# The response matrices on SyncE's queue, and the first MLP's last two down chunks as one seven-product pair

## The chip, the cores and the metric

The kernel runs on one core of one Trainium2 chip. The metric is the device time of one execution in microseconds, lower being better. Before the change three runs gave 2769.85, 2770.20 and 2771.99 us, a median of 2770.2 us.

Five engines work side by side, each in the order of its own instructions: TensorE (PE in the profile, with its weight loads as PEld), VectorE (DVE), ScalarE (ACT), GpSimd (POOL) and SyncE (SP). Transfers between main memory and the on-chip buffer are issued by an engine, here by SyncE or GpSimd, and carried out by 16 DMA engines that all queues share.

## The reference, cut to what matters

Two decoder layers on 256 tokens of width 2048, all in float32. Each layer is `x + mixer(norm(x))`, then `x + memory_attention(norm(x), norm(mem))`, then `x + mlp(norm(x))`; a final norm follows. Two places matter here: the MLP of layer 0 and the mixer of layer 1 right behind it.

```python
def squared_relu_mlp(h, w_up, w_down):          # 2048 -> 8192 -> 2048
    return jnp.square(jax.nn.relu(h @ w_up)) @ w_down

def s5_glu(h, w_in, ...):                       # mixer of layer 1
    u = (h @ w_in).reshape(bsz, seq, 128, 16)   # 128 groups of 16 channels
    ...                                         # 64 complex states a group
    states = lax.associative_scan(combine, (a, bu), axis=0)
    y = jnp.einsum('gcp,sbgp->bsgc', cmat, states).real + d_skip * u
    y = gelu(y)
    val, gate = jnp.split(y @ w_out + b_out, 2, axis=-1)
    return val * sigmoid(gate)
```

## The kernel before

**Products.** Every float32 weight tile of 512 KB (two k tiles of 128 rows by 512 columns, `KB = 2`, `NB = 512`) is loaded by SyncE into a buffer `wraw` (`wload`, L117; four buffers, and a fifth one in the first MLP), cut by ScalarE into a high part `whi` (L103) and by VectorE into a low part `wlo` (L104; three buffers each), and then used by TensorE in 12 matmuls: two k tiles, two token halves, three partial products (high by high, low by high, high by low). `tick` (L83) runs after each such tile. Work that is to be emitted some tiles later is handed to `at(delay, fn)` (L78), which counts in ticks.

**The order on the engines** isn't the order of the source: a scheduler places the instructions by priority, which is the order of emission unless `later` or `high_priority` changes it. `issue_after(self.fed)` keeps a SyncE transfer behind the last weight load that was emitted.

**The first MLP** (`mlp`, L678, layer 0). The 8192 hidden features come in four blocks. For each block the up product makes four chunks of 512 features (`gemm_feat`, L163, squared ReLU at L697), and the down product adds four chunks `n` of 512 output columns onto `x`. In layer 0 each down chunk is `gemm_hid` (L901): 8 weight tiles, 96 matmuls, then two `gather` calls (L720) that add the two token halves to `x`. In the last block, `nxt.start()` (L718) makes the buffer of the next norm, and `nxt.chunk(x, n)` (L744) squares, turns and scales chunk `n` of `x` one tick after it is complete. So the next mixer finds `hT`, its transposed and split input.

**Seven products instead of eight.** The second MLP and the attention's output product already do two chunks at once in `gemm_seven` (L784): of 16 k tiles, four are taken as a 2 by 2 block product with seven instead of eight half-tile products. Before them VectorE forms differences of raw weight tiles (`run`), and sums of activations (`token_sums`, L748: four sums, then the split). Each product has 6 matmuls. Partial results are copied out by `keep` and added by `gather`. The pair holds two accumulators from its start.

**Activation buffers.** `self.act` has two buffers of 32 KB a partition, for whatever is tagged `act`. During the first MLP one holds its input `hT`, and the other `room`, the workspace of the state-space preparation (`ssm_prep`, L1004), which runs beside the MLP and ends with the writes of `Kd` (L1226).

**The state-space mixer** (`s5`, L1259). The input product takes 32 weight tiles (`b_w_in`), four chunks `n` of 8 tiles each, then the output product takes 64 (`b_w_out`). Beside it, per chunk `n`, run small products with matrices that the preparation wrote to main memory: `pq` (4 transfers of 512 KB), `qq` (4 of 512 KB) and the response matrices `dq`. A response matrix is a tile of 128 partitions with a triangle in it, so it is fetched (L1293) as four transfers of 32, 64, 96 and 128 KB, each into 32 partitions:

```python
load(bass.AP(tensor=kd.tensor, offset=kd.offset + 6 * P,
             ap=[[P, 2], [(2 * T - 1) * P, 16], [1, 2 * (h + 1) * P]]),
     t[32 * h:32 * h + 32, 2 * (3 - h) * P:])
```

There are four such matrices a chunk, 16 transfers, 1.25 MB, and 64 transfers in all. They have one set of four tiles (`resp`, L1276), so those of chunk `n` can come only when the products of chunk `n - 1` have read theirs. `load` issues on GpSimd unless `stream` is true, and for `dq` it never is: `pq` and `dq` are GpSimd's, `qq` and the weights SyncE's. `follow(n)` (L1412) hands the work of chunk `n` to `at`; it is called at tick 8(n + 1) of the mixer. The products with `dq` (L1384) and `qq` (L1392) are in `outputs(n, half)`, 14 and 16 ticks later.

Of the kernel before, what the change touches and what calls it, by code (L numbers as in the profile page):

```python
# [9 lines left out]
F32 = mybir.dt.float32  # L10
F32R = mybir.dt.float32r
# [5 lines left out]
P = 128  # L17
# [21 lines left out]
class Trunk:  # L39
# [638 lines left out]
    def mlp(self, x, layer, cur, nxt):  # L678
        nc, a, tc = self.nc, self.a, self.tc
        wu, wd = a["f_w_up"][layer], a["f_w_down"][layer]  # L680
        hT = cur.act
        with tc.tile_pool(name="ml", bufs=4, reuse_waits="tile") as mp:
            r2 = mp.tile([P, 32 if layer else 24], F32, name="r2", bufs=1)[:, 0:2]
            ws = lambda: mp.tile([P, KB * NB], F32, name="ws", bufs=4)
            run = lambda: mp.tile([P, KB * NB], F32, name="run", bufs=1)
            kept = lambda i: more[:, 6 + i // 2, i % 2 * NB:i % 2 * NB + NB]
            self.fifth = None if nxt.closing else mp
            for b in range(DFF // D):
                hid = []
                for n in range(NCH):  # L690
                    h = mp.tile([P, 4, S], F32R, name="hh")
                    l = mp.tile([P, 4, S], F32R, name="hl")
                    rs = []
                    for i in range(2):
                        r = mp.tile([P, 2, S], F32, name="r", bufs=2)
                        self.gemm_feat(hT, wu, 2 * (NCH * b + n) + i, r)
                        nc.vector.scalar_tensor_tensor(out=r, in0=r, scalar=0.0, in1=r, op0=ALU.max, op1=ALU.mult)  # L697
                        self.split(h[:, 2 * i:2 * i + 2], l[:, 2 * i:2 * i + 2], r)
                        rs.append(r)
                    hid.append((h, l))  # L700
                    if nxt.closing and n == 0:
                        sums = []
                    if nxt.closing and n < 2:
                        sums.append(self.token_sums(ws(), lambda: mp.tile([P, 4, 2, P], F32R, name="sums", bufs=4), *rs))
                    if nxt.closing and n == NCH - 2:
                        more = self.act.tile([P, 8, KB * NB], F32, name="more", tag="act")
                        ahead = [self.block_ahead(more, wd, 2 * j, b * KT, j) for j in range(1 if b == DFF // D - 1 else 2)]
                        ahead[0][-2]()
                if nxt.closing:
                    ahead[0][-1](0, 1, 2)  # L710
                if nxt.closing:
                    own = lambda: mp.tile([P, KB * NB], F32R, name="own", bufs=2)
                    nxt.room = lambda: mp.tile([P, 2, NB], F32, name="g", tag="ws", bufs=4)
                if b == 0:
                    rstd = cur.rstd()
                    nc.vector.tensor_tensor(out=r2, in0=rstd, in1=rstd, op=ALU.mult)
                if b == DFF // D - 1 and not nxt.closing:
                    nxt.start()  # L718

                def gather(t, n, part, cs=None):  # L720
                    xc = x[:, t, cs or slice(n * NB, (n + 1) * NB)]
                    nc.vector.scalar_tensor_tensor(out=xc, in0=part, scalar=r2[:, t:t + 1], in1=xc,
                                                   op0=ALU.mult, op1=ALU.add)

                for n in range(NCH):
                    end = b == DFF // D - 1
                    if nxt.closing and not (end and n >= NCH - 2):
                        if n % 2 == 0:
                            self.gemm_seven((ws, run, kept), lambda kt, t: [f[:, kt % 4, t * P:(t + 1) * P]
                                                                            for f in hid[kt // 4]],  # L730
                                            sums, wd, n, b * KT, gather, own=own, ahead=ahead[n // 2],
                                            then=ahead[1] if n == 0 and len(ahead) > 1 else None)
                            if end:
                                nxt.start()
                    elif nxt.closing and end and n == NCH - 1:
                        self.gemm_last(hid, wd, n, b * KT, lambda t, acc: nxt.finish(x, t, lambda cs: gather(
                            t, n, acc[:, cs.start - n * NB:cs.stop - n * NB], cs)))
                        break
                    else:
                        acc = self.gemm_hid(hid, wd, n, b * KT)  # L740
                        for t in range(2):
                            gather(t, n, acc[:, t, :])
                    if end:
                        self.at(4 + n if nxt.closing and n < 2 else 1, lambda n=n: nxt.chunk(x, n))  # L744

            self.fifth = None

# [256 lines left out]
    def ssm_prep(self, pool):  # L1004
# [32 lines left out]
        bbs = [home(4 * 2 * 16).rearrange("p (g k c) -> p g k c", g=4, k=2) for _ in range(4)]  # L1037
        qts = [home((T + 1) * 4 * 16).rearrange("p (w g c) -> p w g c", g=4, c=16) for _ in range(4)]
        pos = [home(4 * 2 * 64).rearrange("p (t r s) -> p t r s", t=4, r=2) for _ in range(4)]
        kds = [home(NL * 2 * 16).rearrange("p (w i c) -> p w i c", i=2, c=16) for _ in range(2)]  # L1040

        def cmul(orr, oi, ar, ai, br, bi):
# [49 lines left out]
        def zoh():  # L1092
            lr, li = e["lr"], e["li"]
            pr, pi = e["pw"][1]
            fr, fi = pool.tile(W, F32, name="fr", tag="w2"), pool.tile(W, F32, name="fi", tag="w3")
            nr, den = pool.tile(W, F32, name="nr", tag="w7"), pool.tile(W, F32, name="den", tag="w9")
            v.tensor_tensor(out=den, in0=lr, in1=lr, op=ALU.mult)
            v.tensor_tensor(out=nr, in0=li, in1=li, op=ALU.mult)
            v.tensor_tensor(out=den, in0=den, in1=nr, op=ALU.add)
            v.reciprocal(out=den, in_=den)  # L1100
            v.tensor_scalar(out=nr, in0=pr, scalar1=-1.0, scalar2=None, op0=ALU.add)
            v.tensor_scalar(out=li, in0=li, scalar1=-1.0, scalar2=None, op0=ALU.mult)
            cmul(fr, fi, nr, pi, lr, li)
            v.tensor_tensor(out=fr, in0=fr, in1=den, op=ALU.mult)
            v.tensor_tensor(out=fi, in0=fi, in1=den, op=ALU.mult)
            pt = self.ps([P, 4, P])
            for k, t in enumerate((fr, fi)):
                nc.tensor.transpose(pt[:, k, :], t, self.ident)
            nc.scalar.copy(out=F, in_=pt[:, 0:2, :])
            e["f"] = fr[:, 0:64], fi[:, 0:64]  # L1110
            lk = pool.tile([P, 2, 64], F32, name="lk")
            for k in range(2):
                nc.scalar.copy(out=lk[:, k], in_=e["f"][k])
            nc.gpsimd.dma_start(out=Ld[0], in_=lk)
            row(1)

        def row(k):
            lk = pool.tile([P, 2, 64], F32, name="lk")
            cmul(lk[:, 0], lk[:, 1], *(f[:, 0:64] for f in e["pw"][k]), *e["f"])
            nc.gpsimd.dma_start(out=Ld[k], in_=lk)  # L1120

# [137 lines left out]
    def s5(self, x, cur, nxt):  # L1259
# [3 lines left out]
        with tc.tile_pool(name="s5", bufs=2, reuse_waits="tile") as sp:  # L1263
# [17 lines left out]
            def fetch(nm, n, i, stream=False):  # L1281
# [5 lines left out]
                elif nm == "qq":  # L1287
                    t = sp.tile([P, 2, 4 * P], F32, name=nm, bufs=4)
                    load(self.Qd[4 * n + i].rearrange("l p r n -> (l p) r n"), t, stream)
                else:  # L1290
                    t, kd = resp[i], self.Kd[4 * n + i]
                    for h in range(4):
                        load(bass.AP(tensor=kd.tensor, offset=kd.offset + 6 * P,  # L1293
                                     ap=[[P, 2], [(2 * T - 1) * P, 16], [1, 2 * (h + 1) * P]]),
                             t[32 * h:32 * h + 32, 2 * (3 - h) * P:])
                ahead[nm, n, i] = t

            def chunks(n, acc):
# [113 lines left out]
            def follow(n):  # L1412
# [3 lines left out]
                for i in range(4):  # L1416
                    if n + 1 < NCH:
                        self.at(5, lambda i=i: fetch("pq", n + 1, i))
                    if n:
                        self.at(7 + late + i // 2 * 2, lambda i=i: fetch("dq", n, i))  # L1420
                        self.at(10 + late + i // 2 * 2, lambda i=i: fetch("qq", n, i, True))
                self.at(4 + late, lambda: inputs(n))
                self.at(6 + late, lambda: states(n))
                self.at(7 + late, lambda: [carry(n, 2, 15), carry(n, 4, 7, 2)])
# [8 lines left out]

            for i in range(4):
                fetch("pq", 0, i)
            for i in range(4):
                fetch("dq", 0, i)
                self.at(2 * i + 2, lambda i=i: fetch("qq", 0, i, True))
            for n in range(NCH):
                acc = self.gemm_tok(hT, a["b_w_in"], n)  # L1440
                if n == 0:
# [227 lines left out]
```

## Time and profile before

| | us |
|---|---|
| median of three runs | 2770.2 |
| the profiled execution | 2772.35 |
| its span, from the first to the last instruction | 2770.2 |
| TensorE busy | 2748.3 |
| VectorE busy | 2066.9 |
| ScalarE busy | 1426.7 |
| GpSimd busy | 184.9 |

The profile covers one execution; its span lacks 2.15 us at the two ends. "Busy" is the time in which an engine had an instruction at work. In the views of the trace, a row of the timeline has the start, the length and the number of like instructions in a row, and in square brackets the idle time before them with what ended it. A row of the windows has the busy time of each engine with the number of its instructions, the granted share of TensorE's clock, the mean busy share of the 16 DMA engines, and the rate.

### The profile page before, as it was taken

The page shows a single profiled execution, that of the slowest core. Times are in us where ns is not written, and L with a number is a line of the kernel's source. Part 1 is how long each engine was busy: PE and PEld are TensorE (multiplying, and loading weights), DVE is VectorE, ACT ScalarE, POOL GpSimd, SP SyncE. Part 2 cuts the span into 40 slices and gives each one's busy share as a digit, 9 for nine tenths or more (in the row PEclk, how much of TensorE's full clock was granted, in tenths as well). Part 3 has the DMA queues.
Part 4 walks back from the last instruction along what each step waited for, and adds up shares of the span by engine and source line. Part 5 has one row for each costly group of instructions (what it writes and reads, how often), then busy time and mean ns, then how long its engine had stood idle before and what let it go on. Part 6 is the DMA issues. An engine that isn't in the chain of part 4 may idle for free. (4 is left out here: it accounts for less than half of the span.)

```text
span 2770.2 us, 39500 instructions
## 1 busy us (share of the span) xinstructions
PE 2748.3 (99%) x14966; PEld 2325.4 (84%) x14966; DVE 2066.9 (75%) x2835; ACT 1426.7 (51%) x1822; POOL 184.9 (7%) x331
## 2 busy tenths in 40 slices
PE   9999999999999999999999999999999999999998
PEld 7888888888888888888888788888888888888887
DVE  6865757878888878787577657568767978879685
ACT  5545545655544434444566445446555655546454
POOL 0100000001011111111203100000000000000000
PEclk9999999999999999999999999999999999999999
DMA  8766566457688887886879766564556557575565
GB/s 293 231 199 214 189 193 217 152 160 238 211 281 259 262 258 257 265 259 219 235 239 284 207 203 206 188 213 156 181 165 231 180 171 241 158 246 166 176 212 160
DMA packets 194175, 593.75 MB, mean 214 GB/s; under 512 B 44096, under 2 KB 45168, under 8 KB 193472
## 3 DMA queue, kind: packets, MB, share of 16 engines
q1 hardware_dynamic: 153456, 537.46, 61.1%
q0 software_dynamic: 40000, 52.71, 6.6%
q8 instruction: 117, 1.92, 0.3%
q10 hardware_dynamic: 528, 1.06, 0.1%
q14 instruction: 74, 0.61, 0.1%
HBM read 567.51 MB, written 23.46 MB: 213 GB/s over the span
## 5 line engine op out<-in xcount | busy, mean ns | idle before, releaser
L104 DVE TENSOR_TENSOR wlo<-wraw,whi 128x1024 fp32r<-128x1024 f32 (+1 forms) x857 | 1041.0, 1220 | 434.8 <-ACT whi L103 429.0
L103 ACT CAST whi<-wraw 128x1024 fp32r<-128x1024 f32 (+1 forms) x857 | 899.4, 1051 | 800.2 <-PE acc L910 172.1
L174 PE MATMUL acc<-act,whi 128*128 128x512 f32 x3072 | 740.9, 391 | 0.6 <-DVE act L246 0.6
L174 PEld LDWEIGHTS acc<-act,whi 128*128 128x128 f32 x3072 | 563.1, 188 | 110.6 <-issue 1.4
L179 PEld LDWEIGHTS acc<-act,wlo 128*128 128x128 f32 x3072 | 395.0, 191 | 17.4 <-DVE wlo L104 1.8
L179 PE MATMUL acc<-act,wlo 128*128 128x256 f32 x3072 | 403.3, 283 | 1.3 <-DVE wlo L104 1.0
L159 PE MATMUL acc<-whi,act 128*128 128x512 f32 x1472 | 370.4, 393 | 5.6 <-ACT whi L103 5.5
L159 PEld LDWEIGHTS acc<-whi,act 128*128 128x128 f32 x1472 | 275.2, 189 | 63.6 <-ACT whi L103 6.3
L810 PE MATMUL acc<-whi,act 128*128 128x512 f32 x824 | 222.7, 392 | 0.0
L910 PE MATMUL acc<-whi,hl 128*128 128x512 f32 x544 | 212.7, 391 | 0.0
L909 PE MATMUL acc<-whi,hh 128*128 128x512 f32 x544 | 212.6, 391 | 0.0
L159 PE MATMUL acc<-wlo,act 128*128 128x512 f32 x736 | 197.9, 391 | 0.0
L810 PEld LDWEIGHTS acc<-whi,act 128*128 128x128 f32 x824 | 152.9, 188 | 35.9 <-ACT ends L846 2.2
L159 PEld LDWEIGHTS acc<-wlo,act 128*128 128x128 f32 x736 | 138.6, 188 | 28.9
L912 PE MATMUL acc<-wlo,hh 128*128 128x512 f32 x544 | 145.8, 389 | 0.0
L810 PE MATMUL acc<-wlo,act 128*128 128x512 f32 x412 | 127.2, 391 | 0.2
L190 ACT COPY r<-acc 128x512 f32<-128x512 f32 x64 | 37.6, 587 | 161.9 <-PE acc L174 161.9
L910 PEld LDWEIGHTS acc<-whi,hl 128*128 128x128 f32 x544 | 102.1, 188 | 22.2 <-issue 1.0
L810 PE MATMUL acc<-whi,hh 128*128 128x512 f32 x308 | 120.5, 391 | 0.0
L909 PEld LDWEIGHTS acc<-whi,hh 128*128 128x128 f32 x544 | 102.1, 188 | 21.4 <-issue 0.2
L912 PEld LDWEIGHTS acc<-wlo,hh 128*128 128x128 f32 x544 | 102.0, 188 | 21.4 <-issue 0.2
L810 PE MATMUL acc<-whi,hl 128*128 128x512 f32 x308 | 119.9, 389 | 0.0
(387 smaller groups left out, 2951.3 us busy)
## 6 DMA issues: line engine op xcount, KB each, us to landing
wraw<-in_f_w_up SPq DMA_DIRECT2D x256, 512.0 KB, 4.5
wraw<-in_f_w_down SPq DMA_DIRECT2D x200, 512.0 KB, 5.6
wraw<-in_x_w_q SPq DMA_DIRECT2D x64, 512.0 KB, 3.7
wraw<-in_x_w_k SPq DMA_DIRECT2D x64, 512.0 KB, 4.5
wraw<-in_b_w_out SPq DMA_DIRECT2D x64, 512.0 KB, 4.5
wraw<-in_a_w_in SPq DMA_DIRECT2D x63, 512.0 KB, 4.7
wraw<-in_x_w_o SPq DMA_DIRECT2D x48, 512.0 KB, 4.3
wraw<-in_x_w_v SPq DMA_DIRECT2D x40, 512.0 KB, 3.9
```

Source lines behind the costliest of these rows:

```text
L103: self.nc.scalar.copy(out=hi, in_=src)
L104: return self.nc.vector.tensor_tensor(out=lo, in0=src, in1=hi.bitcast(F32), op=ALU.subtract).ins
L159: nc.tensor.matmul(out[t], a[:, kt, sl], b[:, kk, :], start=st and a is ah, stop=en)
L174: nc.tensor.matmul(acc[:, f, :], hi[:, kk, sl], both[:, kt].rearrange("p a s -> p (a s)"), start=first and kk == 0, stop=last and kk == FK ...
L179: nc.tensor.matmul(acc[:, f, 0:S], lo[:, kk, sl], ah[:, kt, :], start=False, stop=last and kk == FK - 1, skip_group_check=True)
L190: nc.scalar.copy(out=dst, in_=acc[:, :, S:])
L810: mm = lambda s, m, e: nc.tensor.matmul(out, s, m, start=key not in begun, stop=e, skip_group_check=True)
L909: nc.tensor.matmul(acc[:, t, :], ah, hi[:, kk, :], start=kt == 0, stop=False)
L910: nc.tensor.matmul(acc[:, t, :], al, hi[:, kk, :], start=False, stop=False)
L912: nc.tensor.matmul(acc[:, t, :], hid[kt // 4][0][:, kt % 4, sl], lo[:, kk, :], start=False, stop=kt == KT - 1)
```

## The change

Three things are done. In the last block of the first MLP, the down chunks 2 and 3 go through `gemm_seven` as one pair; its four raw tiles are loaded into a new `act` tile `more` when chunk 1 begins, the sums of activations are formed after the block's first up chunk with `self.spare` (a stretch of `room`) as workspace, and the norm's chunk 3 is handed on with a delay of 2 ticks. In the mixer, the `dq` transfers go to SyncE's queue, and `dq` and `qq` get new ticks: for chunk 0, 6, 8, 14, 16 and three ticks after each; for the others 12 and 14, and one tick after each. Two small preparation tiles share a buffer (`w9`).

```diff
@@ mlp @@
-            ws = lambda: mp.tile([P, KB * NB], F32, name="ws", bufs=4)
-            run = lambda: mp.tile([P, KB * NB], F32, name="run", bufs=1)
+            if nxt.closing:
+                ws = lambda: mp.tile([P, KB * NB], F32, name="ws", bufs=4)
+                run = lambda: mp.tile([P, KB * NB], F32, name="run", bufs=1)
+            else:
+                ws, run = None, lambda: more[:, 4]
...
-                    if nxt.closing and n == 0:
+                    if n == 0:
                         sums = []
-                    if nxt.closing and n < 2:
-                        sums.append(self.token_sums(ws(), lambda: mp.tile([P, 4, 2, P], F32R, name="sums", bufs=4), *rs))
+                    if nxt.closing and n < 2 or not nxt.closing and n == 0 and b == DFF // D - 1:
+                        sums.append(self.token_sums(ws() if nxt.closing else self.spare, lambda: mp.tile([P, 4, 2, P], F32R, name="sums", bufs=4 if nxt.closing else 2),
+                                                    *rs))
...
                 if b == DFF // D - 1 and not nxt.closing:
+                    more = self.act.tile([P, 8, KB * NB], F32, name="more", tag="act")
+                    early = {}
                     nxt.start()
...
+                    elif end and n >= NCH - 2 and not nxt.closing:
+                        if n % 2 == 0:
+                            self.gemm_seven((ws, run, kept), lambda kt, t: [f[:, kt % 4, t * P:(t + 1) * P]
+                                                                            for f in hid[kt // 4]],
+                                            sums, wd, n, b * KT, gather, raw=early)
                     else:
+                        if end and n == 1:
+                            for i, j in ((0, 0), (0, 1), (1, 0), (1, 1)):
+                                t = early[i, j] = more[:, 2 * i + j]
+                                with tc.issue_after(self.fed):
+                                    nc.sync.dma_start(out=t.rearrange("p (k c) -> p k c", k=KB),
+                                                      in_=wd[2 + j, b * KT // KB + i])
                         acc = self.gemm_hid(hid, wd, n, b * KT)
...
-                        self.at(4 + n if nxt.closing and n < 2 else 1, lambda n=n: nxt.chunk(x, n))
+                        self.at(4 + n if nxt.closing and n < 2 else 1 if n < 3 else 2, lambda n=n: nxt.chunk(x, n))
@@ ssm_prep @@
+        self.spare = home(KB * NB)
...
-            lk = pool.tile([P, 2, 64], F32, name="lk")
+            lk = pool.tile([P, 2, 64], F32, name="lk", tag="w9")
@@ s5 @@
-                        load(bass.AP(tensor=kd.tensor, offset=kd.offset + 6 * P,
+                        load(stream=stream, src=bass.AP(tensor=kd.tensor, offset=kd.offset + 6 * P,
                                      ap=[[P, 2], [(2 * T - 1) * P, 16], [1, 2 * (h + 1) * P]]),
-                             t[32 * h:32 * h + 32, 2 * (3 - h) * P:])
+                             out=t[32 * h:32 * h + 32, 2 * (3 - h) * P:])
...
-                    if n:
-                        self.at(7 + late + i // 2 * 2, lambda i=i: fetch("dq", n, i))
-                        self.at(10 + late + i // 2 * 2, lambda i=i: fetch("qq", n, i, True))
+                for k, nm in enumerate(("dq", "qq")) if n else ():
+                    for i in range(4):
+                        self.at(12 + i // 2 * 2 + k, lambda nm=nm, i=i: fetch(nm, n, i, True))
...
-            for i in range(4):
-                fetch("dq", 0, i)
-                self.at(2 * i + 2, lambda i=i: fetch("qq", 0, i, True))
+            for k, nm in enumerate(("dq", "qq")):
+                for i in range(4):
+                    self.at((6, 8, 14, 16)[i] + 3 * k, lambda nm=nm, i=i: fetch(nm, 0, i, True))
```

More of the change, by code (lines that the diff above doesn't have):

```diff
@@ L1117, in row @@
         def row(k):
-            lk = pool.tile([P, 2, 64], F32, name="lk")
+            lk = pool.tile([P, 2, 64], F32, name="lk", tag="w9")
             cmul(lk[:, 0], lk[:, 1], *(f[:, 0:64] for f in e["pw"][k]), *e["f"])
```

## The prediction

> **What bounds the kernel now.** First the page's head and busy times, then who waited for whom on TensorE.
>
> ```profile
> span 2770.2 us, 39500 instructions
> PE 2748.3 (99%) x14966; PEld 2325.4 (84%) x14966; DVE 2066.9 (75%) x2835; ACT 1426.7 (51%) x1822; POOL 184.9 (7%) x331
> PE acc L159 <- ACT whi L103: 5.5, 1, 5.5
> PE ps L1384 <- DMA dq<-Kd: 2.5, 2, 1.9
> PE ps L1337 <- ACT us L1324: 1.7, 2, 0.9
> ```
>
> TensorE is busy for 99% of the span. Apart from the start (5.5 us), which the change doesn't touch, its longest wait is for response matrices, in the mixer. The timeline of TensorE shows the price: the last half of chunk 2 without a wait, then the last half of chunk 3 with it.
>
> ```profile
> 1523.08 1.07 PE L159 MATMUL acc<-wlo,act 128*128 128x512 f32 x4
> ...
> 1528.18 1.07 PE L159 MATMUL ps<-wlo,act 128*128 128x512 f32 x4
> ...
> 1552.88 1.07 PE L159 MATMUL ps<-wlo,act 128*128 128x512 f32 x4
> 1554.56 0.65 PE L1384 MATMUL ps<-dq,us 128*32 128x128 f32 x16 [0.61 <-DMA dq<-Kd]
> 1557.06 0.80 PE L1384 MATMUL ps<-dq,us 128*32 128x128 f32 x16 [1.85 <-DMA dq<-Kd]
> ...
> 1562.15 1.07 PE L159 MATMUL acc<-wlo,act 128*128 128x512 f32 x4
> ```
>
> From one weight tile's low products to the next's, with a half of `outputs` between, take 1528.18 - 1523.08 = 5.10 us undisturbed and 1562.15 - 1552.88 = 9.27 us with the wait: it costs 4.17 us, more than the 2.46 idle, since the matmuls behind it run slower at first.
>
> **The change part by part.**
>
> *Seven products.* One weight tile is 12 matmuls:
>
> ```profile
> 1297.14 0.39 PE L909 MATMUL acc<-whi,hh 128*128 128x512 f32 x1
> ...
> 1299.87 0.39 PE L909 MATMUL acc<-whi,hh 128*128 128x512 f32 x1
> L810 PE MATMUL acc<-whi,act 128*128 128x512 f32 x824 | 222.7, 392 | 0.0
> 1294.00:1316.00 22.00, 22.00 (x105) 17.98 (x107) 11.61 (x11) 9.96 (x11) 0.00 (x0) 1.00 0.65 195
> 2083.43 0.50 PE L179 MATMUL acc<-act,wlo 128*128 128x256 f32 x2 [0.34 <-ACT act L245]
> ```
>
> A tile takes 1299.87 - 1297.14 = 2.73 us, a matmul 0.2275, and not the 0.39 of its row, for matmuls overlap. Two chunks by `gemm_hid` are 16 tiles, 192 matmuls; the pair is 12 tiles and 7 products of 6, 186. Six less are 1.37 us. VectorE gets three more splits and four differences, some 8 us in a stage of about 44, where it is busy for 11.61 of 22; the same pairs elsewhere (L810) leave TensorE without idle time. What can be lost: the norm's chunks 2 and 3 now both come at the end, as behind the attention's last pair, where 0.34 us were waited. I take 1.0 us of gain net, between 0 and 1.37. The sums of activations and the shared small buffer lie beside the up product: nothing, with about 2.5 us if VectorE had no room.
>
> *Raw tiles sooner.* Four transfers of 512 KB stand before chunk 1's weights, 2 MB more at a time when the DMA share is 0.65. ScalarE's casts wait here for TensorE, not for weights:
>
> ```profile
> 1310.04 1.05 ACT L103 CAST whi<-wraw 128x1024 fp32r<-128x1024 f32 x1 [1.67 <-PE acc L910]
> wraw<-in_f_w_down SPq DMA_DIRECT2D x200, 512.0 KB, 5.6
> ```
>
> With five buffers of 2.73 us a weight tile is asked for up to 13.6 us before its cast and lands after 5.6, so 8 us are spare; 2 MB at the rates below are 6 us. I count nothing, 3 us if the cover is short. That `more` takes the buffer of `hT`, and the next norm's `act` that of `room`, may hold the first turned chunk for some 2 us, behind which a whole chunk of matmuls lies.
>
> *The response matrices on SyncE.* GpSimd loses 64 issues, which are off the path. What counts is how these transfers run. The DMA issues, and single landings of the first three transfers that GpSimd issued from 1525.0 on (32, 64 and 96 KB):
>
> ```profile
> Qd<-room POOLq DMA_DIRECT2D x32, 256.0 KB, 12.0
> Pd<-room POOLq DMA_DIRECT2D x32, 256.0 KB, 6.2
> DMA to landing us min/median/max: 3.1/3.1/3.1
> DMA to landing us min/median/max: 4.0/4.0/4.0
> DMA to landing us min/median/max: 5.0/5.0/5.0
> ```
>
> Each 32 KB more cost 0.95 us: 34 GB/s. Such a transfer is narrow: with a single engine's rate below (20 to 25), it has about two of the 16 engines. `Qd`, whose outer dimension is 2 like that of `dq`, needs twice the time of `Pd` for the same bytes. On GpSimd this was harmless, because SyncE's weights passed by. What narrow transfers do in SyncE's own queue is seen once, where three `lb` of 256 KB (outer dimension 8) are issued close together: SyncE's timeline, the windows from 745 and 766, and the landing of the weight tile issued at 746.54.
>
> ```profile
> 742.58 0.62 SPq L1168 DMA_DIRECT2D lb<-Ld  x1
> 743.34 0.35 SPq L127 DMA_DIRECT2D wraw<-in_f_w_down  x1
> 743.80 0.62 SPq L1168 DMA_DIRECT2D lb<-in_b_pc  x1
> 744.47 0.69 SPq L1168 DMA_DIRECT2D lb<-Ld  x1
> 746.54 5.44 SPq L127 DMA_DIRECT2D wraw<-in_f_w_down  x4
> 745.00:747.00 2.00, 2.00 (x13) 1.74 (x12) 2.00 (x3) 0.62 (x1) 0.00 (x0) 1.00 0.45 68
> 766.00:768.00 2.00, 2.00 (x11) 1.65 (x10) 2.00 (x6) 1.06 (x1) 0.83 (x1) 1.00 0.51 109
> DMA to landing us min/median/max: 12.2/12.2/12.2
> ```
>
> With several of them outstanding only half of the DMA time is used (0.45 and 0.51): they don't spread, they queue on the same eight engines, and the weights behind need 12.2 us instead of 5.6, for a tile has landed only when its last sixteenth has. So I take it that the `dq` queue on the same two engines, each tile of weights behind them.
>
> The sum for one of the two, from SyncE's seventh load of the mixer, before which the first `dq` now stands, to the last products of chunk 3:
>
> ```profile
> 1367.03 17.21 SPq L127 DMA_DIRECT2D wraw<-in_b_w_in  x6
> 763.00:764.00 1.00, 1.00 (x6) 0.84 (x5) 1.00 (x3) 0.96 (x4) 0.00 (x0) 1.00 0.87 346
> 1390.00:1400.00 10.00, 10.00 (x46) 8.26 (x44) 6.72 (x19) 4.22 (x4) 0.00 (x0) 1.00 0.93 355
> 1540.00:1550.00 10.00, 10.00 (x132) 8.01 (x131) 4.48 (x4) 2.98 (x3) 1.76 (x3) 1.00 1.01 318
> ```
>
> - `dq`: 16 matrices x 320 KB / 2 = 2560 KB
> - weights of the 42 tiles 6 to 47: 42 x 512 / 16 = 1344 KB
> - `qq`: 16 x 512 / 16 = 512 KB; `pq` of chunks 1 to 3: 12 x 512 / 16 = 384 KB
>
> Together 4800 KB, 4.92 MB. An engine's rate, from the three windows, is 346 / 0.87 / 16 = 24.9 GB/s at best, 355 / 0.93 / 16 = 23.9, or 318 / 1.01 / 16 = 19.7: 198, 206 or 250 us. Before, this stretch lasted from 1384.2 (1367.03 + 17.21) to 1557.9 (1557.06 + 0.80), 173.7 us. So it becomes 24 to 76 us longer. I take 23.9, 32 us: the ten microseconds of that window are the longest fast stretch, and the other engines stand idle meanwhile. To it come three turns at which the one set of tiles must first be read: 3.1 - 0.95 = 2.15 us each before a landing, 6.5 in all. That makes 38.5 us; the old 4.17 us is within the 173.7. Below, the price is bounded by transfers that spread after all: then the wait goes, -4.17.
>
> The Trainium skill says in "DMA: Bandwidth & Descriptors", section "Why a DMA increments its semaphore by 16 and not by 1", that the number of engines is the largest up to 16 that divides the outermost dimension on both sides (2 here, 8 for `lb`), that SyncE's transfers always take the lowest-numbered of them, and that GpSimd's go round. By that rule the sum above stands. The trace agrees on the width (34 GB/s, 0.45); which engines they are no row here shows.
>
> **Sum.** +38.5 - 1.0 = +37.5 us. The profiled execution took 2772.35 us, its span and 2.15 around it, 0.08% over the median 2770.2; from the median the forecast is 2807.7, say **2808 us**. Its own range is 2792 (24.9 GB/s, no time for the turns, the pair's full 1.37) to 2853 (19.7 GB/s, the turns, no gain by the pair).
>
> **The rivals.**
>
> 1. *The transfers spread, or change engines.* Then SyncE issues them without the long wait for earlier landings that GpSimd had, `dq` is there before 1554, the 4.17 us go, the pair gives 1.0 and the norm's end takes 0.3 back: 2770.2 - 4.9 = 2765.3, faster, with 2762.6 if the 1.7 us for `us` go too. It decides at three engines: 173.7 us x 23.9 GB/s are 4150 KB in 1000 bytes, 4054 in 1024, less the 2240 of the rest leaves 1814 KB for `dq`, and 5120 / 1814 = 2.8. For it speaks that SyncE mostly waits for buffers; against it the shares 0.45 and 0.51. The skill's same page, section "Issuing engines are not separate DMA queues", holds that the issuing engine saves only its own issue time; by that rule alone this rival is the result, but its sentence isn't about narrow transfers, and no run here has moved one.
> 2. *Late weights shift ScalarE's copies.* The transfers spread, but casts wait for weights and delay the copies that TensorE waits for, at 0.9 us each (longest of L1337). Four more such waits eat most of the gain: about 2769 us, the same.
> 3. *The change doesn't do what it says.* The last matrices still land late, as each must wait for chunk 2's products: only the pair remains, 2769.2 us, the same.
>
> **How the numbers follow.** The forecast has 0.62, rival 1 has 0.28, rivals 2 and 3 have 0.05 each. A measurement of this kernel tells some 0.2%, 5.5 us, from no change. Rival 1 lies near that bound: 0.13 beyond it, 0.15 within. So slower 0.63 (a little of rival 2), same 0.24, faster 0.13. The range must reach to rival 1: 2764 to 2845 leaves about 0.1 out on either side.
>
> **What would show it.** Right: TensorE waits in the mixer grow to some 40 us, on casts of late weights (L159) and on `dq` (L1384); weights land after 15 us and more between 1390 and 1600, while the DMA share there falls well below its 0.9 to 1.0; `b_w_out` begins later. The first MLP's down stage is a little over 1 us shorter and has no new wait. Wrong: `dq` that land within 6 us on SyncE, and no cast that waits for weights; then rival 1 holds. A wait for `act` or L246 of over 1 us at the mixer's start would show that I cost the pair's end too low.

## The result, and the profile after

The changed kernel takes **2842.5 us** (median of four runs, 2841.7 to 2843.5) against 2770.0 us before: the ratio is 1.0263, with a 95% interval of 1.0247 to 1.0279. It is 72.5 us slower. The forecast was 2808, with a range of 2764 to 2845: the way and the range were right, the loss is nearly twice the 37.5 us that were forecast.

First the head of the page of the profile after: TensorE's busy time grew by 14 us although it has six matmuls less, and its share of the span fell in three slices.

```profile
span 2840.0 us, 39525 instructions
PE 2762.2 (97%) x14960; PEld 2333.7 (82%) x14960; DVE 2080.4 (73%) x2851; ACT 1431.5 (50%) x1830; POOL 147.2 (5%) x267
PE   9999999999999999999986699999999999999998
PEclk9999999999999999999998799999999999999999
```

Those slices are the mixer. TensorE's waits from 1381 to 1625 us (in total, times, longest), where the kernel before had 4.6 us of waits in all:

```profile
PE ps L159 <- ACT whi L103: 15.4, 1, 15.4
PE ps L1355 <- ACT us L1342: 14.1, 3, 12.4
PE ps L1371 <- ACT z L1359: 13.5, 1, 13.5
PE acc L159 <- ACT whi L103: 7.0, 3, 3.4
PE ps L1341 <- ACT u L1330: 5.0, 2, 3.5
```

No row names a transfer, and only two name a cast of weights. Whoever stops here would look for slow copies (`us`, `z`, `u`). ScalarE works in order, though, so one asks what stood ahead of the copy. ScalarE's timeline at the waits of 13.5 and 12.4 us, then TensorE's, first a tile undisturbed, then at the first of the two waits:

```profile
1497.62 1.09 ACT L1342 COPY us<-ps 128x512 f32<-128x512 f32 x2
1518.82 1.04 ACT L103 CAST whi<-wraw 128x1024 fp32r<-128x1024 f32 x1 [20.10 <-DMA wraw<-in_b_w_in]
1519.77 1.19 ACT L1359 COPY z<-ps 128x256 f32<-128x256 f32 x4
...
1567.75 1.04 ACT L103 CAST whi<-wraw 128x1024 fp32r<-128x1024 f32 x1 [16.13 <-DMA wraw<-in_b_w_out]
```

```profile
1399.47 1.98 PE L159 MATMUL acc<-whi,act 128*128 128x512 f32 x8
...
1520.46 1.97 PE L1371 MATMUL ps<-ident,z 128*128 128x128 f32 x8 [13.52 <-ACT z L1359]
1522.08 3.74 PE L159 MATMUL acc<-whi,act 128*128 128x512 f32 x8
```

The copy `z` stood behind a cast that waited 20.1 us for its weights. The wait of 12.4 us for `us` is of the same kind, behind a cast that waited 16.1 us. ScalarE's waits for weights between 1380 and 1640 us, before and after:

```profile
ACT whi L103 <- DMA wraw<-in_b_w_out: 9.2, 4, 3.5
ACT whi L103 <- DMA wraw<-in_b_w_in: 3.0, 2, 1.7
```

```profile
ACT whi L103 <- DMA wraw<-in_b_w_in: 54.4, 12, 20.1
ACT whi L103 <- DMA wraw<-in_b_w_out: 51.3, 8, 24.5
```

They grew from 12.2 to 105.7 us. Now why the weights were late: SyncE's timeline around that cast (its tile is the one issued from 1496.47 on), SyncE's wait before it issues weights, and the windows.

```profile
1484.00 12.38 SPq L1290 DMA_DIRECT2D dq<-Kd  x8
1496.47 2.33 SPq L127 DMA_DIRECT2D wraw<-in_b_w_in  x1
```

```profile
SPq L127 <- DMA dq<-Kd: 27.4, 14, 3.8
```

```profile
1490.00:1498.00 8.00, 6.52 (x32) 4.88 (x30) 4.47 (x8) 4.66 (x9) 0.00 (x0) 1.00 0.13 51
1500.00:1516.00 16.00, 5.62 (x120) 3.94 (x111) 0.27 (x1) 0.00 (x0) 1.33 (x3) 0.77 1.02 316
1517.00:1521.00 4.00, 0.54 (x3) 0.54 (x4) 1.11 (x1) 2.14 (x5) 0.00 (x0) 0.50 0.14 57
1381.26:1619.37 238.11, 177.19 (x1585) 141.29 (x1583) 121.22 (x273) 95.61 (x178) 6.29 (x12) 0.87 0.60 183
```

For eight microseconds, with several transfers of `dq` outstanding, the mean share of the DMA engines is 0.13 at 51 GB/s. Two of 16 are 0.125: **two engines work at 25.5 GB/s each, and fourteen stand idle**. Several outstanding transfers don't raise the share, so they all use the same two. The tile of weights issued at the end of this stretch needs all engines; from 1500 on they are all busy (GpSimd's `pq` of 2 MB is among it), and from 1517 again only about two are at work, on what is left of that tile and of those behind it. It is cast at 1518.82. By the Trainium skill, "DMA: Bandwidth & Descriptors", section "Why a DMA increments its semaphore by 16 and not by 1", a transfer uses as many engines as the largest number up to 16 that divides its outermost dimension on both sides, 2 here; the 0.13 agrees. The windows bear out that the two are always the same; that they are the lowest-numbered ones no row shows. A second path has the same cause: SyncE waited 27.4 us for `dq` to land before it could issue weights at all.

The last window also shows the clock: a granted share of 0.87 over the mixer, 0.50 in the window from 1517. After a wait of 13.5 us, eight matmuls of a tile take 3.74 us instead of 1.98. The Trainium skill, "TensorE: Matmul & The Clock Gate", section "HAM oscillation — how this bites in real kernels", has it that gaps of more than some 3.4 us make TensorE start again at the lower clock. The trace agrees for the wait of 13.5 us; where the limit lies was not tried here.

### The profile page after: what moved, and what is told of

Read it like the earlier page. It is cut to its first block, busy times and chain, and to the rows that moved or that the text cites. A ratio compares the mean times of both kernels' runs of the same rounds, so it can differ in the third digit from the quotient of the medians.

```text
span 2840.0 us, 39525 instructions
## 1 busy us (share of the span) xinstructions
PE 2762.2 (97%) x14960; PEld 2333.7 (82%) x14960; DVE 2080.4 (73%) x2851; ACT 1431.5 (50%) x1830; POOL 147.2 (5%) x267
## 5 line engine op out<-in xcount | busy, mean ns | idle before, releaser
L159 PE MATMUL acc<-whi,act 128*128 128x512 f32 x1472 | 377.4, 399 | 16.8 <-ACT whi L103 12.5
L827 PE MATMUL acc<-whi,act 128*128 128x512 f32 x824 | 222.6, 392 | 0.0
L929 PE MATMUL acc<-wlo,hh 128*128 128x512 f32 x480 | 128.7, 389 | 0.0
L827 PE MATMUL acc<-wlo,hh 128*128 128x512 f32 x362 | 111.5, 389 | 0.0
L927 PEld LDWEIGHTS acc<-whi,hl 128*128 128x128 f32 x480 | 90.1, 188 | 19.7 <-issue 1.0
L926 PEld LDWEIGHTS acc<-whi,hh 128*128 128x128 f32 x480 | 90.1, 188 | 19.0 <-issue 0.2
```

Source lines behind the costliest of these rows:

```text
L159: nc.tensor.matmul(out[t], a[:, kt, sl], b[:, kk, :], start=st and a is ah, stop=en)
L827: mm = lambda s, m, e: nc.tensor.matmul(out, s, m, start=key not in begun, stop=e, skip_group_check=True)
L926: nc.tensor.matmul(acc[:, t, :], ah, hi[:, kk, :], start=kt == 0, stop=False)
L927: nc.tensor.matmul(acc[:, t, :], al, hi[:, kk, :], start=False, stop=False)
L929: nc.tensor.matmul(acc[:, t, :], hid[kt // 4][0][:, kt % 4, sl], lo[:, kk, :], start=False, stop=kt == KT - 1)
```

## The experiments

Each was timed beside the kernel before on the same chip, whose median there was 2769.1 to 2770.4 us. A transfer is called narrow when its outermost dimension is 2, and wide when it is 16. The theories: **A**, narrow transfers on SyncE fill the same two DMA engines, and weights wait there; **B**, it is SyncE's order and the number of its issues; **C**, it is the new ticks.

### The parts of the change, one at a time

`e4_pair_only` is the kernel before with the MLP's part alone.

> The kernel before with the first MLP's part alone: the seven-product pair, its early loads and the shared buffers; response matrices and ticks as before. The prediction's term: 1.0 us less than before, between 0 and 1.37, so 2768.6 to 2770.2 us, and no new wait between the up product and the mixer. Rival: the early loads or the norm's end cost what the pair saves or more, 2770 to 2773 us.

Measured: 2768.1 us, ratio 0.9994 (0.9985 to 1.0002), half a microsecond below the range that was expected and 1.1 under the 2769.1 beside it. What the pair gives is within the measurement's noise; the profile gives it below.

`e3_queue_only` is the other part alone, at the old ticks:

```diff
-load(bass.AP(tensor=kd.tensor, ...
+load(stream=stream, src=bass.AP(tensor=kd.tensor, ...
...
-self.at(7 + late + i // 2 * 2, lambda i=i: fetch("dq", n, i))
+self.at(7 + late + i // 2 * 2, lambda i=i: fetch("dq", n, i, True))
...
-    fetch("dq", 0, i)
+    fetch("dq", 0, i, True)
```

> The kernel before with one edit: the response matrices are issued by SyncE, at the old ticks; no pair. Theory A: two engines carry 2560 KB more than the others whatever the tick, so most of the loss comes, 2820 to 2850 us. Theory C (the new ticks ask too late): asked for five ticks sooner, they are there in time; 2764 to 2772 us.

Measured: 2853.4 us, 1.0301 (1.0286 to 1.0315). It is over A's range by 3 us. C falls: at the old ticks the loss is even some 10 us larger than at the new ones. SyncE's timeline, TensorE's wait and ScalarE's:

```profile
1383.25 17.61 SPq L1272 DMA_DIRECT2D dq<-Kd  x16
```

```profile
PE acc L159 <- ACT whi L103: 59.4, 3, 22.6
```

```profile
ACT whi L103 <- DMA wraw<-in_b_w_in: 53.1, 5, 29.5
```

All four matrices of a chunk go in one row here, 16 transfers, 1.31 MB: at the 51 GB/s that the window from 1388 to 1394 has here too, 25.7 us for two engines. The longest wait of a cast is 29.5 us, and TensorE waits 59.4 us in three pieces; 11.2 us more are waits for `qq`, which is on the same queue. The changed kernel, which asks for two matrices at a time, has smaller heaps.

`e2_gpsimd` is the changed kernel with `dq` back on GpSimd:

```diff
-load(stream=stream, src=bass.AP(tensor=kd.tensor, ...
+load(bass.AP(tensor=kd.tensor, ...
```

> The changed kernel, with the response matrices issued by GpSimd again, at the new ticks. Theory A: no weight waits any more, but the new ticks ask for the matrices of chunks 1 to 3 five ticks (13.6 us) later than before, and on GpSimd's queue they took 13 us to land: waits for dq of up to some 8 us a chunk can take the place, 2768 to 2795 us. Theory B: SyncE's order is as before, so the same range. Theory C (the new ticks are the cause, whatever the queue): 2830 us or more.

Measured: 2769.9 us, 1.0000 (0.9991 to 1.0009). With one queue changed, all 72 us are gone. The new ticks cost nothing that can be measured.

`e11_pair_late` has the pair without its early loads; the raw tiles are asked for where the pair begins.

> The kernel before with the pair, but the four raw tiles asked for where the pair begins, and not a chunk sooner. If the early loads are worth something, TensorE waits at the pair's start for their landing (5.6 us each for weights) and for VectorE's first difference: 2770 to 2776 us. If they are not, as SyncE runs some 13 us ahead of TensorE anyway: 2767 to 2769 us, the same as the pair with them (2768.1).

Measured: 2775.3 us, 1.0020 (1.0011 to 1.0029): 7.2 us more than with the early loads, and by the ratios (1.0020 against 0.9994) the same. TensorE's waits from 1290 to 1385, of which the changed kernel has none:

```profile
PE acc L923 <- DVE wlo L104: 2.0, 1, 2.0
PE acc L821 <- DVE wlo L104: 1.7, 1, 1.7
```

Without the early loads the pair costs more than it saves.

### Width or number of issues

`e1_wide` keeps queue, ticks and bytes, and doubles the number:

```diff
-for h in range(4):
-    load(stream=stream, src=bass.AP(tensor=kd.tensor, offset=kd.offset + 6 * P,
-                 ap=[[P, 2], [(2 * T - 1) * P, 16], [1, 2 * (h + 1) * P]]),
-         out=t[32 * h:32 * h + 32, 2 * (3 - h) * P:])
+for h in range(4):
+    for r in range(2):
+        load(stream=stream, src=bass.AP(tensor=kd.tensor, offset=kd.offset + (6 + r) * P,
+                                        ap=[[(2 * T - 1) * P, 16], [1, 2 * (h + 1) * P]]),
+             out=t[32 * h + 16 * r:32 * h + 16 * r + 16, 2 * (3 - h) * P:])
```

> The changed kernel, with each response-matrix transfer cut into two of 16 partitions, so that its outermost dimension is 16 and not 2: 128 transfers instead of 64, same bytes, same queue, same ticks. Theory A (narrow transfers on SyncE fill the same two DMA engines, and the weights behind them wait there): the stretches with a DMA share of 0.13 go, and with them nearly all of the 72 us; 2764 to 2772 us. Theory B (SyncE's order is the cause: each of these transfers costs some 0.6 us of issue and may wait for an earlier one to land, and the weights are issued behind it): twice the transfers cost at least as much, 2840 us or more.

Measured: 2799.8 us, 1.0111 (1.0092 to 1.0131). Neither number. B is refuted in its strict form, since twice the issues cost 43 us less; A said 2764 to 2772. The transfers themselves now land fast, and ScalarE's wait for weights is 23.1 us instead of 105.7. The DMA issues and ScalarE's waits:

```profile
dq<-Kd SPq DMA_DIRECT2D x32, 64.0 KB, 2.2
```

```profile
ACT whi L103 <- DMA wraw<-in_b_w_out: 23.1, 8, 7.8
```

What is left is seen where TensorE first stands still, at 1405.6. ScalarE's timeline, SyncE's, and the window:

```profile
1396.52 1.05 ACT L103 CAST whi<-wraw 128x1024 fp32r<-128x1024 f32 x1 [1.66 <-PE acc L159]
1406.52 1.22 ACT L1331 ACTIVATE u<-acc,rstd 32x128 f32<-32x128 f32 x4 [8.94 <-DVE u L1328]
1407.77 1.04 ACT L103 CAST whi<-wraw 128x1024 fp32r<-128x1024 f32 x1
```

```profile
1398.86 13.89 SPq L127 DMA_DIRECT2D wraw<-in_b_w_in  x3
```

```profile
1405.00:1411.00 6.00, 2.69 (x8) 1.88 (x7) 3.72 (x7) 4.38 (x10) 0.00 (x0) 0.77 0.00 0
```

No DMA engine does anything. ScalarE's next cast stands behind the copies of `u`, which need the last product of chunk 0; until then no weight is cut, no buffer comes free, and SyncE can't load. In the changed kernel three more casts stand ahead of those copies. So the program's order on ScalarE, which the scheduler writes and which came out another way with 128 transfers on SyncE, made a new wait. The run had changed two things at once; a clean test has to keep the order.

`e5_even_narrow` and `e6_even_wide` have equal transfers, 64 of 64 KB, and differ in width (the first diff is the narrow one's, the second the wide one's; each leaves out a part of every matrix):

```diff
-ap=[[P, 2], [(2 * T - 1) * P, 16], [1, 2 * (h + 1) * P]]), out=t[32 * h:32 * h + 32, 2 * (3 - h) * P:])
+ap=[[P, 2], [(2 * T - 1) * P, 16], [1, 4 * P]]), out=t[32 * h:32 * h + 32, 4 * P:])
```

```diff
-ap=[[P, 2], [(2 * T - 1) * P, 16], [1, 2 * (h + 1) * P]]), out=t[32 * h:32 * h + 32, 2 * (3 - h) * P:])
+ap=[[(2 * T - 1) * P, 16], [1, 8 * P]]), out=t[32 * h:32 * h + 16])
```

> The changed kernel, with all 64 response-matrix transfers made equal: 64 KB each into 32 partitions, 512 columns, outermost dimension 2 as before (a part of each matrix is not loaded, so the output is not the reference's). To be set against the next run, which has the same number of transfers and the same bytes and differs in width alone. Theory A (two engines): 2048 KB of response matrices on each of two engines instead of 2560, together 4288 KB, 4.39 MB; at the 20.8 GB/s that they averaged in the changed kernel (4.92 MB in 237 us) 211 us instead of 174, so 2795 to 2830 us, and stretches with a DMA share of 0.13. Theory B (SyncE's order and number of issues): as the changed kernel, 2835 to 2850 us.

> As the run before, but each transfer of 64 KB goes into 16 partitions, 1024 columns, with an outermost dimension of 16 (other parts of the matrices are not loaded; the output is not the reference's). Theory A: 256 KB for each of 16 engines, so no weight waits: no stretch with a DMA share of 0.13, and 2765 to 2800 us; the upper end for ScalarE's order, which in this kernel places two casts fewer ahead of the first copies of u and may cost up to the 30 us that were left with 128 transfers. Theory B: no better than the run before.

Measured: 2816.3 us (1.0167, 1.0153 to 1.0181) and 2788.6 us (1.0066, 1.0052 to 1.0080), both in A's ranges and out of B's. A window of the narrow run, and two of the wide one:

```profile
1478.00:1485.00 7.00, 7.00 (x40) 5.97 (x39) 6.55 (x12) 4.62 (x11) 0.00 (x0) 1.00 0.13 51
```

```profile
1414.00:1417.00 3.00, 3.00 (x15) 2.49 (x14) 2.23 (x4) 2.92 (x7) 0.00 (x0) 1.00 1.02 153
1399.00:1405.00 6.00, 6.00 (x28) 4.99 (x27) 1.85 (x2) 1.05 (x1) 0.00 (x0) 1.00 1.02 403
```

The narrow one has the stretches at 0.13 and 51 GB/s again; the wide one has all engines busy. The two also differ in the length of their rows (2 and 4 KB) and in ScalarE's order. The narrow one's order can be set aside: by the traces it is, instruction for instruction, that of `e2_gpsimd`, which took 2769.9 us. Why the wide one is still 19 us over the kernel before was not separated.

`e9_split` gives the clean answer: SyncE issues one 16-partition half, GpSimd the other.

```diff
+for r in range(2):
+    load(stream=stream and r == 0,
+         src=bass.AP(tensor=kd.tensor, offset=kd.offset + (6 + r) * P,
+                     ap=[[(2 * T - 1) * P, 16], [1, 2 * (h + 1) * P]]),
+         out=t[32 * h + 16 * r:32 * h + 16 * r + 16, 2 * (3 - h) * P:])
```

> The changed kernel, with each response-matrix transfer cut into two of 16 partitions, of which SyncE issues the first and GpSimd the second. SyncE has the same 64 transfers at the same places, and ScalarE's instructions stand in the same order as in the changed kernel; only the width (16 instead of 2) and the other half's queue differ. Theory A (two engines): no stretch with a DMA share of 0.13, ScalarE waits for weights below 30 us instead of 106, and 2765 to 2780 us. Theory B (the 64 issues on SyncE, or the order that the program was given with them): 2830 us or more. In between, some 2800: what is left with 128 transfers on SyncE is neither the width nor the changed order of ScalarE.

Measured: **2765.4 us**, 0.9982 (0.9973 to 0.9991), with SyncE's 64 issues and, by the traces, all 1830 instructions of ScalarE in the changed kernel's order. ScalarE's wait for weights and TensorE's only wait in the mixer:

```profile
ACT whi L103 <- DMA wraw<-in_b_w_out: 9.3, 6, 2.8
```

```profile
PE ps L1343 <- ACT u L1332: 0.2, 1, 0.2
```

So neither the issues nor the order that came with them cost the 72 us. B falls.

GpSimd carries half of the bytes here, though. `e12_split_narrow` is its twin, which has that too, and is cut by columns instead of partitions:

```diff
+m = (h + 1) * P
+load(stream=stream and r == 0,
+     src=bass.AP(tensor=kd.tensor, offset=kd.offset + 6 * P + r * m,
+                 ap=[[P, 2], [(2 * T - 1) * P, 16], [1, m]]),
+     out=t[32 * h:32 * h + 32, 2 * (3 - h) * P + r * m:2 * (3 - h) * P + r * m + m])
```

> The twin of the run with the split transfers: again SyncE issues one half of each response-matrix transfer and GpSimd the other, the same bytes and numbers, but cut by columns, so that each half keeps 32 partitions and the outermost dimension 2. Theory A (two engines): SyncE's halves put 1280 KB on each of two engines, with weights, qq and pq 3520 KB, 3.60 MB; at 20.8 GB/s 173 us, just what the stretch has. So the average no longer decides, but each pair of matrices holds the two engines for 160 KB, 6.4 us at 25.5 GB/s, of the 8 us that the weights have to spare: stretches with a DMA share of 0.13 of some 5 us, small waits for weights, and with GpSimd's narrow halves slower than the wide ones 2768 to 2795 us. Theory B (width doesn't matter): as the wide twin, 2764 to 2767 us.

Measured: 2789.1 us, 1.0070 (1.0058 to 1.0082), in A's range. The same bytes on the same queues, in halves that are wide or narrow, are 23.7 us apart. A window:

```profile
1512.00:1517.00 5.00, 5.00 (x28) 4.24 (x27) 4.85 (x12) 3.29 (x7) 0.00 (x0) 1.00 0.15 52
```

TensorE's waits are 19.6 us, 16.6 of them for `us`. With half the bytes the stretch is about 5 us, as worked out. ScalarE's order differs in five places between the twins, but the narrow one's is again that of `e2_gpsimd`, so it isn't what costs the 23.7 us. Its rows are half as long as the wide twin's (0.5 to 2 KB instead of 1 to 4); still 52 GB/s are moved at a share of 0.15.

### Eight engines, and a better kernel

`e7_square` fetches each matrix whole in one transfer with an outermost dimension of 8; `e8_square_gp` does so on GpSimd, in the kernel with the pair alone.

```diff
+load(stream=stream, src=bass.AP(tensor=kd.tensor, offset=kd.offset,
+                                ap=[[P, 8], [(2 * T - 1) * P, 16], [1, T * P]]), out=t)
```

> The changed kernel, with each response matrix fetched whole, zeros included, as one transfer of 512 KB whose outermost dimension is 8: 16 transfers instead of 64 on SyncE, 8.4 MB instead of 5.2 MB, no clearing of the tiles. Theory A: 64 KB of it for each of eight engines, 1024 KB and not 2560 in all; with weights, qq and pq 3264 KB, 3.34 MB at 20.8 GB/s are 161 us, under the 174 us that the stretch has: no wait for weights of over 2 us, 2763 to 2772 us. A rival: 3 MB more in a stretch whose DMA share is 0.87 already make weights late; 2775 to 2800 us.

> The kernel before with the pair, and the whole response matrices of the run before issued by GpSimd at the old ticks. 16 transfers instead of 64 on GpSimd, each wide, so that none waits for earlier ones. Theory A: the matrices land within some 8 us as pq does, the waits for dq go (2.5 us of idle time in the kernel before, 2.6 with the pair alone), 2763 to 2767 us. Rival: 3 MB more in the stretch delay other transfers by as much; 2768 to 2775 us.

Measured: 2799.7 us (1.0103, 1.0088 to 1.0119) and 2778.2 us (1.0030, 1.0020 to 1.0040). A's numbers failed in both; the first is within its rival's, the second above both. Two windows of `e7_square`:

```profile
1461.00:1470.00 9.00, 9.00 (x127) 7.43 (x116) 8.45 (x37) 5.86 (x12) 0.00 (x0) 1.00 1.03 166
1489.00:1493.00 4.00, 0.00 (x0) 0.00 (x0) 0.49 (x1) 1.57 (x3) 0.00 (x0) 0.50 0.51 200
```

The second shows the width once more: with an outermost dimension of 8 there is a stretch with a share of 0.51 and 200 GB/s, eight engines at 25 (whether on matrices or on tiles queued behind them, the row doesn't tell). The first shows what A's sum lacked: while whole matrices, weights and `qq` are outstanding together, all engines are busy and move only 166 GB/s, 10 a piece. The sum took one rate for all bytes. On GpSimd, where the matrices were expected within some 8 us, they landed after 20.2 us (median).

`e10_wide_gp` leaves SyncE alone: the pair, and transfers of 16 partitions on GpSimd at the old ticks.

> The kernel before with the pair, and the response matrices in transfers of 16 partitions issued by GpSimd at the old ticks: 128 issues of 0.5 us on an engine that is busy for 7%. Theory A: the matrices land in some 3 to 5 us instead of 13, so the waits for dq (2.6 us of idle time with the pair alone) go: 2763 to 2767 us. Rival: GpSimd's issues wait for earlier landings as before, and TensorE for the last matrices: 2768 to 2771 us.

Measured: **2765.6 us**, 0.9982 (0.9974 to 0.9991). The matrices land in some 5 us (5.4 for those of 64 KB) instead of 12 to 14. TensorE's only wait in the mixer:

```profile
PE ps L1342 <- ACT u L1331: 0.2, 1, 0.2
```

It and `e9_split` are faster than both kernels: 5 us under the one before, 77 under the changed one. `e10_wide_gp` lies 2.5 us under `e4_pair_only`, by the ratios 3.3; that much is due to the wide transfers, and the rest to the pair.

## Why the prediction was right, and where its size was off

TensorE's timeline before and after: the first down product, the low products of the mixer's eighth tile, its 47th tile, and the low products of a later one.

```profile
1294.42 0.39 PE L909 MATMUL acc<-whi,hh 128*128 128x512 f32 x1
...
1406.80 1.07 PE L159 MATMUL acc<-wlo,act 128*128 128x512 f32 x4
...
1548.22 2.11 PE L159 MATMUL ps<-whi,act 128*128 128x512 f32 x8
...
1593.86 1.07 PE L159 MATMUL acc<-wlo,act 128*128 128x512 f32 x4
```

```profile
1292.44 0.39 PE L926 MATMUL acc<-whi,hh 128*128 128x512 f32 x1
...
1404.00 1.07 PE L159 MATMUL acc<-wlo,act 128*128 128x512 f32 x4
...
1619.37 3.78 PE L159 MATMUL ps<-whi,act 128*128 128x512 f32 x8 [15.42 <-ACT whi L103]
...
1663.33 1.07 PE L159 MATMUL acc<-wlo,act 128*128 128x512 f32 x4
```

**What bounds the kernel.** Right. With the wait for `dq` gone, `e9_split` and `e10_wide_gp` are 5 us under the kernel before; the forecast's terms, 4.17 for the wait and 1.0 for the pair, add up to that, though the runs put some 3 on the wait and 1 to 2 on the pair.

**Seven products, 1.0 us.** Right. The first down product began at 1294.42 before and at 1292.44 after, the low products of the mixer's eighth tile at 1406.80 and 1404.00: 2.80 - 1.98 = 0.82 us by this stage, and no wait in it. (The 1.98 arose before anything that the change touches: 1.97 of it stood at 325 us already, and `e4_pair_only`, with the same pair, has 0.08 there.) The raw tiles sooner were rightly put at nothing; what their lack would cost, 7.2 us, I had not asked.

**The matrices on SyncE.** The mechanism was right: a share far below 0.9 (0.60 over the mixer), casts that wait up to 24.5 us for weights, waits on casts and behind them. Wrong was the guess that TensorE would also wait for `dq` itself; 59.3 of the 60.8 us of waits came through ScalarE. And **the step "I take 23.9" failed**, with the end of its sum.

From the first `dq`, issued at 1382.53, to the 47th tile are 236.8 us. The 4.92 MB of the sum in that time are 20.8 GB/s, not 23.9: 31 us more than the 206. The two engines reach 25.5 GB/s only while they are alone; when all work they get 316 / 16 = 19.8 (window from 1500). Of 237 windows of one microsecond from 1382 on, 71 have a share of 0.08 to 0.20, at 51 GB/s on average, and 106 a share of 0.8 or more, at 18.8 GB/s an engine; 3 have less than 0.08, so the two are hardly ever idle. The rate of 19.7 from the third window was at hand, and I had kept it for the range's end only. Then, the sum was set against 173.7 us up to the last products. But what waits longest is the tile of weights behind the last matrices, and this tile came after 1548.22 - 1384.2 = 164.0 us before: 10 us more. The 6.5 us for turns are within the 236.8. Together 38.5 + 31 + 10 - 6.5 = 73, and 236.8 - 164.0 are 72.8. The range held the result 2.5 us from its upper end, because 19.7 was in it; that the ten microseconds of the wrong end point still fitted was luck. Two sums of the prediction are 1 us off, without weight here: the lower end of its own range adds up to 2793, and rival 1 with the 1.7 us to 2763.6.

Seen from TensorE, the low products of the eighth tile and those at 1593.86 before and 1663.33 after are 187.06 and 259.33 us apart, 72.3 more. Its waits account for 60.8 - 4.6 = 56.2 of these. The other 16 are left for the matmuls at the lower clock; that fits TensorE's busy time, which grew by 14 us with six matmuls less. That second part was in no term of the forecast as such.

**The rivals.** The first, that transfers spread, is false for narrow transfers; its price of 2765.3 us is what two kernels with wide ones take (2765.4 and 2765.6), while two others with wide ones on SyncE alone stayed at 2788.6 and 2799.8. The rule of the Trainium skill, "DMA: Bandwidth & Descriptors", section "Issuing engines are not separate DMA queues", by which the issuing engine saves only its own issue time, doesn't give the price of narrow transfers: between `e2_gpsimd` and the changed kernel, which differ in the issuing engine and in five places of ScalarE's order, lie 2769.9 and 2842.5 us. The second rival's late weights and shifted copies did occur, but because the transfers did not spread, and at far more than its four times 0.9 us; the third did not occur. That it decides at three engines was not tried by itself.

**Open:** what of the 34 us between `e1_wide` and `e9_split` is ScalarE's order, what the 128 issues on SyncE and what the other half's queue, as they came together.

## What to carry to other kernels

Before a transfer is moved to the queue that feeds the weights, look at its outermost dimension on both sides: in these runs it went with how many DMA engines worked (2, 8 or 16), and narrow ones made the weights behind them wait. Cut it into pieces with 16 rows outermost. Here this was worth 43 us with all pieces on SyncE's queue, 77 with half of them given to GpSimd, and some 3 on GpSimd's queue alone. Then compare the order of the other engines' instructions, which the scheduler may have changed. And where TensorE waits for copies, look at what stands ahead of them on their engine before you blame them.

## What was not expected of the hardware

While the scratch matrices were read in rows of 4 KB by 8 or 16 engines (`e7_square`, `e6_even_wide`), beside weights, 153 to 166 GB/s were moved with every DMA engine busy, 10 GB/s each. Without them `e6_even_wide` moved 403, 25 each. Two engines alone got 25 each from the same matrices. What slows it no run here tells: the rows of these transfers overlap in what they read, and many engines read them at the same time.
